# HGRN2 branch of a two-layer hybrid decoder on Trainium2: the local part by doubling blocks of gate products in place of logarithms, scans and exponentials

## Chip, cores and metric

The kernel runs on one NeuronCore of one Trainium2 chip (trn2). Its engines work side by side, each on its own queue of instructions in a fixed order: PE (TensorE: matrix products, with PEld for the loading of their weights), DVE (VectorE), ACT (ScalarE), POOL (GpSimd) and SP (SyncE, which here issues the transfers). The metric is the device time of one execution in microseconds.

## What is computed

The reference is a decoder trunk of two layers on 256 tokens of width 1024. Each layer has a token mixer of three branches (latent attention, gated DeltaNet "dn", HGRN2 "hg"), merged by gates and projected out, and then a mixture of 32 experts. The change lies in the HGRN2 branch of the mixer, which works on 4 heads of 128 channels and in chunks of 64 tokens:

```python
f = lb + (1.0 - lb) * jax.nn.sigmoid(z)
k = (1.0 - lb) * jax.nn.sigmoid(-z)
log_f = jnp.log(jnp.maximum(f, MIN_FORGET))
...
bc = jnp.cumsum(bc, axis=3)
q_dec = qc * jnp.exp(bc)
k_dec = kc * jnp.exp(bc[:, :, :, -1:, :] - bc)
d_last = jnp.exp(bc[:, :, :, -1, :])
...
def step(state, inp):
    dec = masked_exp(tri_incl, bs[:, :, :, None, :] - bs[:, :, None, :, :])
    att = jnp.einsum('bhid,bhjd,bhijd->bhij', qs, ks, dec)
    o = jnp.einsum('bhcd,bhde->bhce', qd, state) + jnp.einsum('bhij,bhje->bhie', att, vs)
    state = state * dl[..., :, None] + jnp.einsum('bhcd,bhce->bhde', kd, vs)
```

The decay between tokens j and i of a chunk is the product of the gates f from j+1 to i, channel by channel. `att` is needed for every pair in a chunk; `q_dec`, `k_dec` and `d_last` hold the products from the chunk's start to a token, from a token to the chunk's end, and over the whole chunk.

## The kernel before

All products are in fp32. Large projections are split into three products of high and low parts: ACT casts a quarter or half of a 1 MB weight tile to its high part `wh` (L249, 128x1024), DVE forms the low part `wl` (L250; at a few places POOL does), and PE runs lines 261, 262 and 263 into a PSUM bank. Activations of the branch are held with channels on partitions and 4 heads x 256 tokens in a row of 1024.

Each layer calls its stages in the order of the string `seq`: `dn_decay`, `mla`, heads, `dn_keys`, `dn_inverse`, `dn_queries`, `dn_values`, `hg_forget`, `hg_project`, `hg_local`, `dn_scan`, `hg_scan`; then the input to the experts, `merge_branch` for "a", the gates, `merge_branch` for "b" and "c", `project_out` and `moe`. That is only the order of the text: a scheduler of the framework sets the order in which instructions stand on each engine, so that PE finds the products of one stage (among them `dn_scan`, L951 to L972, and the projections of `merge_branch`, L261 to L263) between those of another. The order is fixed before the kernel runs; an instruction that waits holds up all behind it on its engine.

`hg_local` (L1011) works in halving blocks. It splits f into two ranges, takes two logarithms (L1022, L1023; a set of activation tables is named at L1021), adds them (L1024) and scans them along each chunk (L1027) to the running sum `b`. `pairs` (L1033) forms, for 4 heads and 4 chunks, the 64x64 products of keys and queries on PE (16 matmuls, L1040), and DVE copies the entries that a mask names into `att` (L1042). It is called seven times: for the diagonal, for blocks of one token (with X = f*q, L1046) and for blocks of 32, 16, 8, 4 and 2 tokens. Each of the last five takes a new tile X: POOL subtracts the block's reference from `b` (L1054, L1055, 512 columns each), ACT takes the exponential (L1056), and DVE multiplies the first half by k (L1057) and the second by q (L1058). At the end POOL, ACT and DVE form the keys for the chunk's state in the same way (L1065 to L1067), PE transposes them (L1072) with copies on ACT (L1073), and ACT and DVE form the decayed queries (L1076, L1077) and the chunk's decay (L1075). `hg_scan` then carries the state through the four chunks (L1094 to L1113).

Behind it, the gates' tanh in `merge_branch` stand at L1289. In `moe`, the router takes exponentials (L1438, L1440), and the tokens that each expert gets are gathered on PE (L1573) and evicted by DVE (L1580) and ACT (L1582). `up` (L1623) and `down` (L1656) are the experts' products. The weights of all stages come through one queue, in order, each tile loaded when a buffer is free: four buffers in the mixer, and eighteen more, opened in steps from the moment at which the mixer's own tiles are given up.

Of the kernel before, what the change touches and what calls it, by code (L numbers as in the profile page):

```python
# [10 lines left out]
F32 = mybir.dt.float32  # L11
# [3 lines left out]
AF = mybir.ActivationFunctionType  # L15
OP = mybir.AluOpType
# [3 lines left out]
DEPTH, D, T = 2, 1024, 256  # L20
# [4 lines left out]
NH = 4  # L25
C = 64
# [81 lines left out]
class Trunk:  # L108
# [357 lines left out]
    def mixer_consts(self, l, mp):  # L466

        nc = self.nc
        self.mconst = mp.tile([128, HOST.shape[1] - KEPT], F32, name="mconst")
        nc.sync.dma_start(self.mconst, self.A["consts"][:, KEPT:])  # L470
        self.ones_r = mp.tile([128, 128], F32R, name="ones")
        one = self.buf("d4", [128, 8, 128])[:, 0]
        nc.gpsimd.memset(one, 1.0)
        nc.gpsimd.tensor_copy(self.ones_r, one)
        self.ones = self.ones_r.bitcast(F32)
        self.scanm = mp.tile([128, T], F32, name="scanm")
        nc.gpsimd.memset(self.scanm, 1.0)
        nc.gpsimd.memset(self.scanm.rearrange("p (n c) -> p n c", c=C)[:, :, 0:1], 0.0)


    def norm_weights(self, l):
# [81 lines left out]
    def router_sums(self, after):  # L563
# [6 lines left out]
        with self.tc.issue_after(after):  # L570
            nc.vector.tensor_reduce(self.rsum, rw.rearrange("p k c -> p c k"), axis=AX.X, op=OP.add)
        nc.vector.tensor_add(self.rsum[0:1, 36:72], self.rsum[0:1, 36:72], self.rb)
# [438 lines left out]
    def hg_local(self, l, mp):  # L1011
        nc = self.nc
        q, k, v, f = self.hq, self.hk, self.hv, self.hf
        fl = lambda x: x.rearrange("p h t -> p (h t)")
        t4 = lambda: self.buf("a4", [128, NH, T])

        lo, g = t4(), t4()
        two60 = 2.0 ** -60
        nc.vector.tensor_scalar(lo, f, 1e-30, two60, op0=OP.max, op1=OP.min)
        nc.vector.tensor_scalar(g, f, two60, None, op0=OP.max)  # L1020
        self.tc.keep_in_program_order(nc.scalar.preload_act_table_set("natural_log_exp_and_others"))  # L1021
        nc.scalar.activation(lo, lo, AF.Ln, scale=2.0 ** 60)  # L1022
        nc.scalar.activation(g, g, AF.Ln)  # L1023
        nc.vector.tensor_add(g, g, lo)  # L1024
        b = t4()
        for h in range(NH):
            nc.vector.tensor_tensor_scan(b[:, h], self.scanm, g[:, h], 0.0, op0=OP.mult, op1=OP.add)  # L1027

        att = self.buf("a2", [128, 8, C])
        nc.gpsimd.memset(att, 0.0)  # L1030
        up, eye = self.cst("uplev"), self.cst("eye64")

        def pairs(xk, xq, m):  # L1033
            ps = self.ps()
            pv = ps.rearrange("p (a i) -> p a i", i=C)
            for t in range(TB):
                for h in range(NH):
                    for c in range(2):
                        o = 128 * t + 64 * c
                        nc.tensor.matmul(pv[64 * c:64 * c + 64, 4 * t + h], xk[:, h, o:o + 64], xq[:, h, o:o + 64],  # L1040
                                         start=True, stop=True)
            nc.vector.copy_predicated(att, m.bitcast(I32)[:, None, :].to_broadcast([128, 8, C]), pv)  # L1042

        pairs(k, q, eye)
        X = t4()
        nc.vector.scalar_tensor_tensor(X, f, 1e-30, q, op0=OP.max, op1=OP.mult)  # L1046
        pairs(k, X, up[:, 0:64])
        for lev in range(5, 0, -1):
            w = 1 << lev
            sp = lambda x: fl(x).rearrange("p (n s w) -> p n s w", s=2, w=w)  # L1050
            X = t4()
            nb = NH * T // (2 * w)
            ref = sp(b)[:, :, 0, w - 1:w].to_broadcast([128, nb, w])
            nc.gpsimd.tensor_tensor(sp(X)[:, :, 0], ref, sp(b)[:, :, 0], op=OP.subtract)  # L1054
            nc.gpsimd.tensor_tensor(sp(X)[:, :, 1], sp(b)[:, :, 1], ref, op=OP.subtract)  # L1055
            nc.scalar.activation(X, X, AF.Exp)  # L1056
            nc.vector.tensor_mul(sp(X)[:, :, 0], sp(X)[:, :, 0], sp(k)[:, :, 0])  # L1057
            nc.vector.tensor_mul(sp(X)[:, :, 1], sp(X)[:, :, 1], sp(q)[:, :, 1])  # L1058
            pairs(X, X, up[:, 64 * lev:64 * lev + 64])
        self.hatt = att  # L1060

        ch = lambda x: fl(x).rearrange("p (n c) -> p n c", c=C)
        last = ch(b)[:, :, C - 1:C]
        X = t4()
        nc.gpsimd.tensor_tensor(ch(X), last.to_broadcast([128, 16, C]), ch(b), op=OP.subtract)  # L1065
        nc.scalar.activation(X, X, AF.Exp)
        nc.vector.tensor_mul(X, X, k)  # L1067
        self.hkd = self.buf("a4", [128, 8, 128])
        for t in range(TB):
            ps = self.ps()  # L1070
            for h in range(NH):
                nc.tensor.transpose(ps[:, 128 * h:128 * h + 128], X[:, h, 128 * t:128 * t + 128], self.ident)  # L1072
            nc.scalar.copy(self.hkd[:, 4 * t:4 * t + 4].rearrange("p h d -> p (h d)"), ps)  # L1073
        self.hdl = self.small([128, 16])
        nc.scalar.activation(self.hdl, last.rearrange("p n c -> p (n c)"), AF.Exp)  # L1075
        nc.scalar.activation(b, b, AF.Exp)  # L1076
        nc.vector.tensor_mul(b, b, q)  # L1077
        self.hqd = b

    def hg_scan(self, l, mp):  # L1080
        nc = self.nc
# [714 lines left out]
```

## Time and profile before

| | us |
|---|---|
| median of three runs | 1173.57 (1173.55 to 1175.22) |
| the profiled execution, its own time | 1175.78 |
| its span, first to last instruction | 1174.0 |
| PE busy (share of the span) | 1070.1 (91%) |
| DVE busy | 592.7 (50%) |
| ACT busy | 450.8 (38%) |
| POOL busy | 178.0 (15%) |
| mean granted TensorE clock | 0.961 of full |

The profile is of one execution. Its times are microseconds from the start of the span unless they are in ns; L1040 is line 1040 of the kernel. A row of the time line gives start, duration, engine, line, operation and tiles, the count of instructions merged into it, and in brackets how long the engine sat idle before it and what ended that. A matmul's duration overlaps with the next one's, so the cost of one is read from the distance between two starts. An fp32 matmul mostly leaves two records. The profile's own "chain that ended last" holds the last 1% of the span alone, so the argument below goes by PE's waits and time lines.

### The profile page before, as it was taken

What the parts mean: (1) busy time and instruction counts of PE and PEld (TensorE: products, weight loads), DVE (VectorE), ACT (ScalarE), POOL (GpSimd) and SP (SyncE); (2) the same over time, 40 slices, a digit from 0 to 9 for tenths busy, and PEclk for the clock granted to TensorE, in tenths of its full rate; (3) what the DMA queues carried; (4) which work ended last, traced back from release to release, by engine and by line L of the source; (5) the groups of instructions that cost most, each with busy time, mean ns of one, the idle gap of its engine ahead of it and who ended that gap; (6) DMA issues with size and microseconds to landing.
All of it is one profiled execution on the core that took longest, in us unless ns stands there. A gap on an engine that the chain in (4) does not pass through costs nothing. (4 is left out here: it accounts for less than half of the span.)

```text
span 1174.0 us, 21469 instructions
## 1 busy us (share of the span) xinstructions
PE 1070.1 (91%) x8896; PEld 776.0 (66%) x8896; DVE 592.7 (50%) x1281; ACT 450.8 (38%) x812; POOL 178.0 (15%) x160
## 2 busy tenths in 40 slices
PE   7999998999999999777899999899999999978775
PEld 5888976777777655444388889667777775644342
DVE  7687648466556323111176775665754563321114
ACT  5764653454444212111077545446444442211111
POOL 2111016401110400000030110470012104000001
PEclk9999998999999999889799999999999999998988
DMA  7631331358985899999983224214499669999995
GB/s 232 199 110 61 109 108 37 122 173 306 419 341 216 335 425 424 427 426 427 399 227 113 74 73 137 80 37 147 159 399 427 233 247 427 424 426 426 427 427 207
DMA packets 104706, 305.58 MB, mean 260 GB/s; under 512 B 20962, under 2 KB 48028, under 8 KB 79516
## 3 DMA queue, kind: packets, MB, share of 16 engines
q1 hardware_dynamic: 104604, 304.15, 67.5%
q8 instruction: 72, 1.18, 0.4%
q14 instruction: 30, 0.25, 0.1%
HBM read 303.08 MB, written 1.05 MB: 259 GB/s over the span
## 5 line engine op out<-in xcount | busy, mean ns | idle before, releaser
L250 DVE TENSOR_TENSOR wl<-w,wh 128x1024 fp32r<-128x1024 f32 x150 | 187.2, 1249 | 157.7 <-ACT wh L249 155.1
L249 ACT CAST wh<-w 128x1024 fp32r<-128x1024 f32 x158 | 165.7, 1049 | 202.5 <-PE ps_pa L263 70.2
L1623 PE MATMUL ps_pa<-w,xg 128*32 128x256 f32 x2304 | 176.7, 437 | 57.2 <-DMA w<-in_exp_w_up_dram 28.3
L1623 PEld LDWEIGHTS ps_pa<-w,xg 128*32 128x32 f32 x2304 | 85.5, 125 | 142.6 <-DMA w<-in_exp_w_up_dram 37.5
L1635 DVE SCALAR_TENSOR_TENSOR hm<-ps_pa,ws,hm 128x256 f32<-128x256 f32 x18 | 8.7, 484 | 203.0 <-ACT hm L1634 202.8
L1634 ACT ACTIVATE hm<-ps_pa 128x256 f32<-128x256 f32 x18 | 6.9, 384 | 221.8 <-PE ps_pa L1623 221.8
L261 PE MATMUL ps_po<-wh,hTh 128*128 128x512 f32 x176 | 71.5, 406 | 2.1 <-ACT hTh L254 0.8
L261 PE MATMUL ps_pa<-wh,hTh 128*128 128x512 f32 x176 | 71.5, 406 | 2.1 <-ACT hTh L254 0.8
L262 PE MATMUL ps_pa<-wl,hTh 128*128 128x512 f32 x176 | 71.1, 404 | 2.1 <-DVE wl L250 1.6
L262 PE MATMUL ps_po<-wl,hTh 128*128 128x512 f32 x176 | 70.9, 403 | 2.1 <-DVE wl L250 1.6
L1656 PE MATMUL ps_pm<-w,hmT 128*32 128x512 f32 x576 | 70.8, 595 | 1.3 <-issue 1.3
L263 PE MATMUL ps_pa<-wh,hTl 128*128 128x512 f32 x176 | 70.9, 403 | 0.2 <-DVE hTl L255 0.2
L263 PE MATMUL ps_po<-wh,hTl 128*128 128x512 f32 x176 | 70.6, 401 | 0.2 <-DVE hTl L255 0.2
L1573 PEld LDWEIGHTS ps_pm<-P,h1c 128*128 128x128 f32 x576 | 66.8, 192 | 2.2 <-ACT res L1371 1.0
L1573 PE MATMUL ps_pm<-P,h1c 128*128 128x128 f32 x576 | 67.4, 275 | 0.1
L1582 ACT ACTIVATE xg<-ps_pm,gb 128x128 f32<-128x128 f32 x72 | 32.9, 458 | 74.7 <-DVE xg L1580 74.7
L1595 POOL TENSOR_TENSOR Pw<-P,small 128x128 f32<-128x128 f32 x32 | 12.4, 406 | 308.2 <-PE ps_pm L1602 231.7
L1300 POOL TENSOR_TENSOR mix<-mix,sg 128x512 f32<-128x512 f32 x16 | 28.3, 1789 | 155.4 <-DVE sg L1298 155.4
L1580 DVE TENSOR_SCALAR xg<-ps_pm,gb 128x128 f32<-128x128 f32 x72 | 29.4, 408 | 41.1 <-PE ps_pm L1573 32.2
L263 PE MATMUL ps_po<-hTh,wl 128*128 128x256 f32 (+1 forms) x168 | 48.8, 290 | 0.8 <-DVE wl L250 0.5
L263 PE MATMUL ps_pa<-hTh,wl 128*128 128x256 f32 (+1 forms) x168 | 48.9, 291 | 0.5 <-DVE wl L250 0.5
L261 PE MATMUL ps_pa<-hTh,wh 128*128 128x256 f32 (+1 forms) x168 | 49.3, 294 | 0.0
(460 smaller groups left out, 2198.1 us busy)
## 6 DMA issues: line engine op xcount, KB each, us to landing
w<-in_exp_w_gate_dram SPq DMA_DIRECT2D x66, 1024.0 KB
w<-in_exp_w_up_dram SPq DMA_DIRECT2D x66, 1024.0 KB
w<-in_exp_w_down_dram SPq DMA_DIRECT2D x64, 1024.0 KB
w<-in_w_in_dram SPq DMA_DIRECT2D x58, 1024.0 KB
w<-in_w_out_dram SPq DMA_DIRECT2D x8, 1024.0 KB
w<-in_w_br_a_dram SPq DMA_DIRECT2D x4, 1024.0 KB
w<-in_w_br_b_dram SPq DMA_DIRECT2D x4, 1024.0 KB
w<-in_w_br_c_dram SPq DMA_DIRECT2D x4, 1024.0 KB
```

Source lines behind the costliest of these rows:

```text
L249: nc.scalar.copy(v(hi), raw)
L250: engine.tensor_tensor(v(lo), raw, v(hi).bitcast(F32), op=OP.subtract)
L261: mm(ps, a[0], b[0], start=start, stop=False, skip_group_check=True)
L262: mm(ps, a[0], b[1], start=False, stop=False, skip_group_check=True)
L263: mm(ps, a[1], b[0], start=False, stop=stop, skip_group_check=True)
L1300: nc.gpsimd.tensor_tensor(mv, mv, sg[t], op=OP.add)
L1573: nc.tensor.matmul(ps[:, 128 * k:128 * k + 128], xc[:, t, 4 * h + k], Ps[q][:, t], start=(t == 0), stop=(t == 1))
L1580: nc.vector.tensor_scalar(xg[:, k], o, g, b, op0=OP.mult, op1=OP.add)
L1582: nc.scalar.activation(xg[:, k], o, AF.Identity, scale=g, bias=b)
L1595: self.pool_last = nc.gpsimd.tensor_tensor(e(Pw[:, t]), e(P[:, t]), w, op=OP.mult)
L1623: nc.tensor.matmul(pg[32 * e:32 * e + 32, FF * n:FF * n + FF], xgs[q][k // 4][:, k % 4, 32 * e:32 * e + 32], w[:, FF * k:FF * k + FF], sta ...
L1656: nc.tensor.matmul(ps[c][32 * e:32 * e + 32], hmT[:, i, 32 * e:32 * e + 32], ws[e][:, D * i + 512 * c:D * i + 512 * c + 512], start=(i == ...
```

## The change

Logarithms, scan and exponentials are gone. Two tiles are kept and grown in place: X starts as q*f and `k` as it is. After the products of a level with blocks of w tokens, POOL multiplies the first half of each pair of blocks in `k` by the gate product of the second block, and DVE multiplies the second half in X by that of the first block; then DVE forms the products `d` for blocks of twice the length. The levels run from 1 to 32 tokens, smallest first. After six of them X is `q_dec`, k is `k_dec` and the last `d` is the chunk's decay. `f` is clamped below once, in place. The number of `pairs` calls (seven) and of PE instructions stays. The set of tables for logarithm and exponential is no longer loaded here. In the changed file the products are at L1025, the masked copy at L1027, the clamp at L1031, X = q*f at L1034, POOL's product at L1044, DVE's at L1045, `d` at L1047 and the transposes at L1056.

```diff
@@ -473,9 +473,6 @@
         nc.gpsimd.memset(one, 1.0)
         nc.gpsimd.tensor_copy(self.ones_r, one)
         self.ones = self.ones_r.bitcast(F32)
-        self.scanm = mp.tile([128, T], F32, name="scanm")
-        nc.gpsimd.memset(self.scanm, 1.0)
-        nc.gpsimd.memset(self.scanm.rearrange("p (n c) -> p n c", c=C)[:, :, 0:1], 0.0)
 
 
     def norm_weights(self, l):
@@ -1014,18 +1011,6 @@
         fl = lambda x: x.rearrange("p h t -> p (h t)")
         t4 = lambda: self.buf("a4", [128, NH, T])
 
-        lo, g = t4(), t4()
-        two60 = 2.0 ** -60
-        nc.vector.tensor_scalar(lo, f, 1e-30, two60, op0=OP.max, op1=OP.min)
-        nc.vector.tensor_scalar(g, f, two60, None, op0=OP.max)
-        self.tc.keep_in_program_order(nc.scalar.preload_act_table_set("natural_log_exp_and_others"))
-        nc.scalar.activation(lo, lo, AF.Ln, scale=2.0 ** 60)
-        nc.scalar.activation(g, g, AF.Ln)
-        nc.vector.tensor_add(g, g, lo)
-        b = t4()
-        for h in range(NH):
-            nc.vector.tensor_tensor_scan(b[:, h], self.scanm, g[:, h], 0.0, op0=OP.mult, op1=OP.add)
-
         att = self.buf("a2", [128, 8, C])
         nc.gpsimd.memset(att, 0.0)
         up, eye = self.cst("uplev"), self.cst("eye64")
@@ -1041,41 +1026,35 @@
                                          start=True, stop=True)
             nc.vector.copy_predicated(att, m.bitcast(I32)[:, None, :].to_broadcast([128, 8, C]), pv)
 
+
+
+        nc.vector.tensor_scalar(f, f, 1e-30, None, op0=OP.max)
         pairs(k, q, eye)
-        X = t4()
-        nc.vector.scalar_tensor_tensor(X, f, 1e-30, q, op0=OP.max, op1=OP.mult)
-        pairs(k, X, up[:, 0:64])
-        for lev in range(5, 0, -1):
+        X, rest = t4(), t4()
+        nc.vector.tensor_mul(X, q, f)
+        self.hdl = self.small([128, 16])
+        d, at = fl(f), 0
+        for lev in range(6):
             w = 1 << lev
+            pairs(k, X, up[:, 64 * lev:64 * lev + 64])
+            n = NH * T // (2 * w)
             sp = lambda x: fl(x).rearrange("p (n s w) -> p n s w", s=2, w=w)
-            X = t4()
-            nb = NH * T // (2 * w)
-            ref = sp(b)[:, :, 0, w - 1:w].to_broadcast([128, nb, w])
-            nc.gpsimd.tensor_tensor(sp(X)[:, :, 0], ref, sp(b)[:, :, 0], op=OP.subtract)
-            nc.gpsimd.tensor_tensor(sp(X)[:, :, 1], sp(b)[:, :, 1], ref, op=OP.subtract)
-            nc.scalar.activation(X, X, AF.Exp)
-            nc.vector.tensor_mul(sp(X)[:, :, 0], sp(X)[:, :, 0], sp(k)[:, :, 0])
-            nc.vector.tensor_mul(sp(X)[:, :, 1], sp(X)[:, :, 1], sp(q)[:, :, 1])
-            pairs(X, X, up[:, 64 * lev:64 * lev + 64])
+            d2 = d.rearrange("p (n s) -> p n s", s=2)
+            over = lambda s: d2[:, :, s, None].to_broadcast([128, n, w])
+            nc.gpsimd.tensor_tensor(sp(k)[:, :, 0], sp(k)[:, :, 0], over(1), op=OP.mult)
+            nc.vector.tensor_tensor(sp(X)[:, :, 1], sp(X)[:, :, 1], over(0), op=OP.mult)
+            dn = self.hdl if lev == 5 else fl(rest)[:, at:at + n]
+            nc.vector.tensor_tensor(dn, d2[:, :, 0], d2[:, :, 1], op=OP.mult)
+            d, at = dn, at + n
         self.hatt = att
 
-        ch = lambda x: fl(x).rearrange("p (n c) -> p n c", c=C)
-        last = ch(b)[:, :, C - 1:C]
-        X = t4()
-        nc.gpsimd.tensor_tensor(ch(X), last.to_broadcast([128, 16, C]), ch(b), op=OP.subtract)
-        nc.scalar.activation(X, X, AF.Exp)
-        nc.vector.tensor_mul(X, X, k)
+        self.hqd = X
         self.hkd = self.buf("a4", [128, 8, 128])
         for t in range(TB):
             ps = self.ps()
             for h in range(NH):
-                nc.tensor.transpose(ps[:, 128 * h:128 * h + 128], X[:, h, 128 * t:128 * t + 128], self.ident)
+                nc.tensor.transpose(ps[:, 128 * h:128 * h + 128], k[:, h, 128 * t:128 * t + 128], self.ident)
             nc.scalar.copy(self.hkd[:, 4 * t:4 * t + 4].rearrange("p h d -> p (h d)"), ps)
-        self.hdl = self.small([128, 16])
-        nc.scalar.activation(self.hdl, last.rearrange("p n c -> p (n c)"), AF.Exp)
-        nc.scalar.activation(b, b, AF.Exp)
-        nc.vector.tensor_mul(b, b, q)
-        self.hqd = b
 
     def hg_scan(self, l, mp):
         nc = self.nc
```

**On PE, first layer, around the last levels.** L1040 (before) and L1025 (now) are the products of `pairs`; L948, L956, L957 and L962 now (L951, L959, L960 and L965 before) belong to `dn_scan`; `hTh`/`hTl` rows are the projection of the first merge gate. Before, the groups for blocks of 32, 16, 8 and 4 tokens:

```order
L262 MATMUL ps_pa<-wl,hTh 128x512
L1040 MATMUL ps_pm<-a_2003 64x64 x16
L1040 MATMUL ps_pm<-a_2027 64x64 x16
L263 MATMUL ps_pa<-wh,hTl 128x512
L261 MATMUL ps_pa<-wh,hTh 128x512
L262 MATMUL ps_pa<-wl,hTh 128x512
L1040 MATMUL ps_pm<-a_2051 64x64 x16
L263 MATMUL ps_pa<-wh,hTl 128x512
L262 MATMUL ps_po<-wl,hTh 128x512
L263 MATMUL ps_po<-wh,hTl 128x512
L261 MATMUL ps_po<-wh,hTh 128x512
L1040 MATMUL ps_pm<-a_2075 64x64 x16
```

Now, the groups for 16 and 32 tokens and the transposes:

```order
L948 MATMUL ps_pb<-d_2148,d_1552 64x128 x4
L956 MATMUL ps_pb<-d_2148,d_1581 64x128
L262 MATMUL ps_po<-wl,hTh 128x512
L263 MATMUL ps_po<-wh,hTl 128x512
L1025 MATMUL ps_pm<-a_1968,a_1619 64x64 x16
L957 MATMUL ps_pb<-d_2151,d_1262 64x128
L956 MATMUL ps_pb<-d_2148,d_1581 64x128
...
L957 MATMUL ps_pb<-d_2151,d_1262 64x128
L1025 MATMUL ps_pm<-a_1968,a_1619 64x64 x16
L962 MATMUL ps_pb<-d_2151,d_744 128x128 x3
L1056 MATMUL ps_pm<-const,a_1619 128x128 x8
```

Before, two groups of `pairs` stood together and one to four products of the projection between the others; now most of `dn_scan` stands between them, and three matmuls stand between the last group and the transposes.

**On DVE, first layer, the first levels.** The masked copy is L1042 before and L1027 now. Before:

```order
L250 TENSOR_TENSOR wl<-w,wh 128x1024
L1042 COPY_PREDICATED a_1963<-mconst,ps_pm 128x512
L1057 TENSOR_TENSOR a_2003<-a_2003,a_1622 128x16x32
L1058 TENSOR_TENSOR a_2003<-a_2003,a_1754 128x16x32
L1057 TENSOR_TENSOR a_2027<-a_2027,a_1622 128x32x16
L1058 TENSOR_TENSOR a_2027<-a_2027,a_1754 128x32x16
L1057 TENSOR_TENSOR a_2051<-a_2051,a_1622 128x64x8
L1042 COPY_PREDICATED a_1963<-mconst,ps_pm 128x512
L1058 TENSOR_TENSOR a_2051<-a_2051,a_1754 128x64x8
```

Now:

```order
L1047 TENSOR_TENSOR a_1969<-a_1969 128x128
L250 TENSOR_TENSOR wl<-w,wh 128x1024
L1027 COPY_PREDICATED a_1947<-mconst,ps_pm 128x512
L1045 TENSOR_TENSOR a_1968<-a_1968,a_1620 128x512
L1047 TENSOR_TENSOR a_1969<-a_1969 128x64
...
L1045 TENSOR_TENSOR a_1968<-a_1968,a_1969 128x256x2
L950 TENSOR_TENSOR d_2126<-d_1551,ps_pb 64x512
L250 TENSOR_TENSOR wl<-w,wh 128x1024
L1027 COPY_PREDICATED a_1947<-mconst,ps_pm 128x512
L1045 TENSOR_TENSOR a_1968<-a_1968,a_1969 128x128x4
```

Now each masked copy stands ahead of the in-place product of X (L1045) that the next group on PE needs, and at two levels L250, the low part of the next projection's weights, stands ahead of both.

**On ACT, at the router of the first layer.** Before:

```order
L1371 ACTIVATE res<-res,small,ln_rs 128x512 x4
L1438 ACTIVATE small<-small 128x4
L1440 ACTIVATE small<-small 128x1
L1438 ACTIVATE small<-small 128x4
L1440 ACTIVATE small<-small 128x1
L1582 ACTIVATE xg<-ps_pm,gb_281 128x128 x4
L1634 ACT_TABLE_LOAD
```

Now:

```order
L1350 ACTIVATE res<-res,small,ln_rs 128x512 x4
L1417 ACT_TABLE_LOAD
L1417 ACTIVATE small<-small 128x4
L1419 ACTIVATE small<-small 128x1
L1417 ACTIVATE small<-small 128x4
L1419 ACTIVATE small<-small 128x1
L1561 ACTIVATE xg<-ps_pm,gb_278 128x128 x4
L1613 ACT_TABLE_LOAD
```

A load of activation tables now stands ahead of the router's exponentials (L1417, L1419; before L1438, L1440). In the mixer three loads are gone: at L1021, L1022 and L1289. The second layer has the same orders.

## Rows read from the trace of the kernel before

**Rows 1.** What the transfers moved, 40 equal slices of the span.

```profile
GB/s 232 199 110 61 109 108 37 122 173 306 419 341 216 335 425 424 427 426 427 399 227 113 74 73 137 80 37 147 159 399 427 233 247 427 424 426 426 427 427 207
```

**Rows 2.** PE's waits, layer 0, 160 to 220: who for whom, total, times, longest.

```profile
PE ps_pm L1040 <- DVE a L1058: 2.9, 2, 1.9
PE ps_pm L1040 <- DVE a L1046: 1.3, 1, 1.3
PE ps_pm L1094 <- ACT a L1073: 0.3, 1, 0.3
PE ps_pa L261 <- ACT sg L1289: 0.2, 1, 0.2
```

**Rows 3.** The same, layer 1, 738 to 796; the other three as in layer 0.

```profile
PE ps_pm L1040 <- DVE a L1058: 4.2, 4, 1.9
```

**Rows 4.** Two windows: busy time of PE, PEld, DVE, ACT, POOL; PEclk; DMA; GB/s.

```profile
182.90:194.10 11.20, 8.30 (x102) 6.85 (x102) 10.05 (x11) 4.47 (x5) 10.91 (x8) 0.54 0.14 52
...
759.30:767.70 8.40, 5.50 (x68) 4.47 (x67) 7.25 (x8) 3.51 (x4) 8.40 (x6) 0.59 0.18 69
```

**Rows 5.** PE's time line, layer 0.

```profile
172.14 0.43 PE L960 MATMUL ps_pb<-d,d 64*64 64x128 f32 x2
172.50 1.16 PE L965 MATMUL ps_pb<-d,d 64*128 64x128 f32 x8
173.58 0.50 PE L263 MATMUL ps_po<-wh,hTl 128*128 128x512 f32 x1
173.92 0.40 PE L261 MATMUL ps_po<-wh,hTh 128*128 128x512 f32 x1
174.15 0.40 PE L262 MATMUL ps_po<-wl,hTh 128*128 128x512 f32 x1
...
188.02 1.98 PE L1040 MATMUL ps_pm<-a 128*64 128x64 f32 x32 [1.03 <-DVE a L1058]
189.93 0.80 PE L263 MATMUL ps_pa<-wh,hTl 128*128 128x512 f32 x1
...
191.51 1.98 PE L1040 MATMUL ps_pm<-a 128*64 128x64 f32 x32
...
194.82 1.15 PE L1040 MATMUL ps_pm<-a 128*64 128x64 f32 x32
...
217.58 0.49 PE L261 MATMUL ps_pa<-wh,o 128*128 128x512 f32 x1 [0.24 <-ACT sg L1289]
```

**Rows 6.** DVE's time line, layer 0.

```profile
165.00 0.73 DVE L1042 COPY_PREDICATED a<-mconst,ps_pm 128x512 f32<-128x512 int32 x1 [3.37 <-POOL wl L250]
...
176.71 1.20 DVE L1046 SCALAR_TENSOR_TENSOR a<-a,a 128x1024 f32<-128x1024 f32 x1
...
186.25 1.63 DVE L1058 TENSOR_TENSOR a<-a,a 128x512 f32<-128x512 f32 x1
...
194.47 1.73 DVE L1057 TENSOR_TENSOR a<-a,a 128x512 f32<-128x512 f32 x1
196.12 0.68 DVE L1058 TENSOR_TENSOR a<-a,a 128x512 f32<-128x512 f32 x1
```

**Rows 7.** POOL's time line, layer 0.

```profile
178.77 2.05 POOL L1055 TENSOR_TENSOR a<-a 128x512 f32<-128x512 f32 x1
180.78 1.03 POOL L971 TENSOR_TENSOR d<-d,small 128x512 f32<-128x512 f32 x1
...
185.74 1.59 POOL L1055 TENSOR_TENSOR a<-a 128x512 f32<-128x512 f32 x1
```

**Rows 8.** ACT's time line, layer 0: a table load, and the router's end.

```profile
166.24 1.28 ACT L1021 ACT_TABLE_LOAD   x1
167.53 1.06 ACT L1023 ACTIVATE a<-a 128x1024 f32<-128x1024 f32 x1
...
379.97 0.46 ACT L1582 ACTIVATE xg<-ps_pm,gb 128x128 f32<-128x128 f32 x1 [1.36 <-DVE xg L1580]
```

**Rows 9.** PE's waits, experts of layer 0, 372 to 572.

```profile
PE ps_pa L1623 <- DMA w<-in_exp_w_gate_dram: 14.7, 9, 1.8
```

## Prediction

> **What bounds the kernel now.** Begin with the engines' shares: PE is busy for 91% of the span, so only what keeps PE waiting or slow can be worth much. Next, what the transfers moved [rows 1]: they run at the most that this trace shows (424 to 427 GB/s) in the stages of the experts and far below it in the mixer. The change lies in the mixer, twice (164 to 218 in layer 0, 740 to 794 in layer 1). There PE's waits are the view to read [rows 2, 3]. In layer 0 PE waits 1.3 us for X = f*q (L1046, which stands behind the scan on DVE), 2.9 us for the products of the levels (L1058), 0.3 for the copy behind the transposes and 0.2 for the tanh behind its table load: 4.7 in all. In layer 1 the waits for L1058 are 4.2 and the rest as before: 6.0.
>
> Then the granted clock [rows 4]: after those waits it is 0.54 of full over 11.2 us and 0.59 over 8.4 us, that is for most of each window at the lower of its two levels (1.2 of 2.4 GHz). What that costs is seen on the time line [rows 5]: a group of `pairs` that lasts 1.15 us at 194.82 lasts 1.98 at 188.02 and at 191.51, 0.83 more. Three groups lie in the slow stretch of layer 0 (2.5 us), and three projection products between 189.93 and 191.51 take 1.58 us where 0.9 would do (0.23 each, 0.1 at each change of kind). With a fifth of a microsecond of others: 3.3 us. Layer 1 by the shorter window, 8.4 of 11.2: 2.5.
>
> So the local part costs PE 8.0 us in layer 0 and 8.5 in layer 1, in waits and low clock. It does so because everything waits for the scan, and because POOL then spends two subtractions a level.
>
> **What goes.** On ACT two logarithms, six full exponentials and a seventh for the queries (1.06 us each, the row at 167.53 [rows 8]) and three table loads of 1.28; on DVE the scan, the sum and 12 products; on POOL eleven subtractions. None of that counts by itself, since only PE's waits and clock were on the path: it is worth the 8.0 and 8.5.
>
> There is a third term, in the order on PE. Between the last ten products for the diagonal and the first product of the branch projection PE changes 25 times between large projection products and small ones before, and 11 times now. A change costs 0.1 us: 173.58 to 173.92 is 0.34, 173.92 to 174.15 is 0.23 [rows 5]. That is 14 times 0.1, 1.3 rounded down. PE's instructions are the same in number and shape, so nothing else changes there.
>
> **What comes: a closed loop.** Before, a level's X was a new tile and levels overlapped. Now `k` and X are grown in place: POOL and DVE may write only when PE has read the level's group, and the next group needs what they wrote. A round on DVE is: a lag (0.14: L1058 at 186.25 ends at 187.88, the group on PE starts at 188.02 [rows 5, 6]), the masked copy, which stands first in DVE's order (0.73), the product of X, a lag again. The product has no row; the nearest are DVE's two-input products over 512 columns, 0.68 alone and up to 1.73 beside POOL [rows 6]. I take 1.1, between them, since POOL works at the same moment. Round: 0.14 + 0.73 + 1.1 + 0.14 = 2.1 us, bounds 1.7 and 2.75. On POOL the product of `k` is bounded by 1.03 and 2.05 [rows 7]; I take 1.5, a round of 1.8, so X is the later one.
>
> What stands on PE between the groups covers this. Unit costs [rows 5]: 0.36 for one matmul of the alternating `dn_scan` rows (172.14 to 172.50), 1.08 for four others (172.50 to 173.58), 0.23 for a projection product. Counted in the new order: after the level of 1 token 2.9 us, of 2 tokens 3.0, of 4 tokens 5.4, of 8 tokens 1.8 (four, one and two products), of 16 tokens 2.5 (seven alternating), and of 32 tokens 0.8 (three, at a quarter of 1.08). Against a round of 2.1 the waits are:
> - after 1 token, 0.4: L250 stands ahead of the masked copy and adds 1.2 (as large as L1046, 1.20 [rows 6]), 3.3 against 2.9;
> - after 2, 4 and 16 tokens none; after 4 tokens L250 stands ahead again, and waits for a cast on ACT that waits for PE, but 5.4 covers the two;
> - after 8 tokens, 0.3;
> - before the transposes, 1.0: 1.8 for POOL's last product against 0.8;
> - behind the transposes, 0.3 for the ACT copy, as now.
>
> Together 2.0 us a layer. With the lower bounds 0.5 (the transposes alone), with the upper ones 4.0 (1.1, 0.95, 0.2, 1.5 and 0.3).
>
> The head of the chain is hidden: X = q*f takes what L1046 took (1.20) and the first `d` products under 1 us each, where DVE sat 3.37 us before the copy at 165.00 [rows 6]. The clamp of f costs less than L1046 and stands behind `hg_forget`, 20 us ahead of its reader; if it delayed L250 there, PE would lose under 1.2. The later `d` are narrower; I cost them at nothing beside the covers above. No transfer moves past another: SP's order is the same, and each weight tile is released by its split, which comes earlier now.
>
> **The load that moves to the router.** The tanh of the merge now runs on the set already loaded, and the router's exponentials need a load of 1.28 us (L1021's row [rows 8]) instead. The eviction of gathered tokens on ACT stands behind it. Before, ACT sat 1.36 us ahead of that for DVE [rows 8], and DVE's new order has other work there first. So I charge 0.15 a layer; uncovered it would be 1.28. The Trainium skill, "ScalarE: Activation LUTs", section "What ACT_TABLE_LOAD costs", gives 1.28 us for the load and 1.38 more for a drain, 2.66 for a switch. This trace shows the load but not the drain: L1023 starts 1.29 us behind it [rows 8]. By the page the router would lose up to 1.3 us a layer more and the time would be 2.6 us longer.
>
> **Sum.** Layer 0: 8.0 + 1.3 - 2.0 = 7.3. Layer 1: 8.5 + 1.3 - 2.0 = 7.8. Less 0.3 for the routers: 14.8 us. What comes behind is the same work in the same order, and its weights are asked for when the mixer's tiles are given up, which moves with PE; so the gain passes through. Against the profiled execution (1175.78): 1161.0. It lies 2.2 above the median of the runs (1173.57), against which I give the number: **1158.8**. With all lower bounds and no loss at the router: 15.1 + 2 x 1.5 = 18.1, 1155.5. With all upper ones (waits of 4.0, router 1.28): 15.1 - 4.0 - 2.6 = 8.5, 1165.1.
>
> **Rivals.**
> - *DVE and POOL take strict turns.* At 185.74 POOL's subtraction takes 1.59 and DVE's product, started at 186.25, ends only at 187.88, 0.55 behind it; alone they take 1.03 and 0.68 [rows 6, 7]. If each simply waits the other out, a round is 0.14 + 1.03 + 0.68 + 0.14 = 2.0 with the masked copy hidden under POOL, and POOL's last product is over in 1.3; the waits fall to 0.1 + 0.2 + 0.5 + 0.1 = 0.9, and the time to 1158.8 - 2.2 = 1156.6. Against it: other rows beside POOL last up to 1.73. The Trainium skill, "SBUF — State Buffer", section "SBUF: two separate sides", states this as a rule: the two engines share a port pair as an exclusive lock, taken for a whole instruction, also by a DVE operation with two SBUF inputs. The rows above agree.
> - *The clock falls all the same.* If the waits after 1 and 8 tokens and ahead of the transposes leave PE at the lower level as now, the 3.3 and 2.5 are paid again, and some 1 more since all groups follow closer: 1158.8 + 7 = 1165.8. For it: a single wait of 1.9 preceded the fall [rows 2]. Against it: my longest is 1.0, and the wait of 1.3 at L1046 left the clock full.
> - *The expert weights swallow it.* Transfers run at 424 to 427 GB/s through most of the experts [rows 1], and PE waits 14.7 us for one kind of weight tile alone [rows 9]. If their stream started at a time of its own, an earlier mixer would only wait longer: 1173.6. Against it: ahead of that stretch they fall to 216 GB/s in a slice, so the buffers are full and the stream resumes when PE frees them.
> - *Slower: the closed loop becomes the bound.* If the in-place products cost their upper rows one after the other (0.73 + 1.73 + 2.05 and two lags, 4.8 a round), PE waits 3.1 + 1.8 + 0 + 3.0 + 2.3 + 3.3 = 13.5 a layer, with six groups at low clock 5.0 more: 18.5 against 9.3 gained, 2 x 9.2 slower, 1192. It decides from a round of about 3.8 us on at full clock, 2.9 with the clock low. Nothing in the rows adds these three up.
>
> **How the numbers follow.** The forecast has 0.55, strict turns 0.20, the low clock 0.13, the swallowed gain 0.07, the closed loop 0.05. The range reaches from 1155.5 to 1166.4: the sum's bounds (1155.5 to 1165.1), which hold strict turns too, and the low clock at 1165.8; it leaves out the last two cases. About 0.2% (2.3 us) can be told from no change: faster is 0.55 + 0.20 + 0.13 = 0.88, same 0.07, slower 0.05.
>
> **What would show it.** PE's waits for L1045 and L1044 should sum to about 1.7 us a layer, the longest ahead of the transposes; the clock should be full from 164 to 210; the first product of the branch projection, at 217.58 now [rows 5], should start near 210; the first expert product should be 7 us earlier in layer 0 and 15 in layer 1. It would be wrong if DVE's round were above 2.75, if the clock fell in spite of short waits, or if PE's waits for expert weights grew by what the mixer saved.

## The result, and the profile after

| | before | after |
|---|---|---|
| device time, median of 4 runs each (lowest, highest) | 1173.69 us (1173.55, 1175.22) | 1158.54 us (1156.85, 1160.61) |
| ratio, with its 95% interval | | 0.9868 (0.9856 to 0.9880) |
| profiled execution: its time, its span | 1175.78, 1174.0 | 1160.61, 1158.8 |

The change makes the kernel 15.15 us faster; 14.8 was forecast. The total hides two errors of opposite sign, so the time line is read in stages first. Each stage is the distance between two starts of rows: POOL's split L250 near 162 (and near 732 in layer 1) and the first branch product on PE (the local part); DVE's L337 and the first projection product, both at the start of layer 1; and the end of the span.

| stage, us | before | after | gain |
|---|---|---|---|
| to POOL's split near 162 | 162.51 | 162.30 | 0.21 |
| local part, layer 0 | 55.07 | 45.69 | 9.38 |
| from there to L337 of layer 1 | 372.24 | 371.03 | 1.21 |
| start of layer 1, L337 to first projection product | 6.78 | 11.35 | **-4.57** |
| from there to POOL's split of layer 1 | 142.31 | 141.96 | 0.35 |
| local part, layer 1 | 55.07 | 45.69 | 9.38 |
| to the end | 380.02 | 380.78 | -0.76 |

The local part gained 2.1 us more than forecast in layer 0 and 1.6 in layer 1. And 4.57 us were given back where the change seems to do nothing. (The third row is no gain of the change: an experiment below with before's order took 370.36 there.)

First the local part. PE's waits of after, layer 0, 160 to 220, answer to [rows 2]:

```profile
PE ps_pm L1056 <- POOL a L1044: 0.4, 1, 0.4
PE ps_pb L948 <- DVE d L969: 0.3, 1, 0.3
PE ps_pm L1025 <- DVE a L1047: 0.3, 1, 0.3
PE ps_pm L1025 <- DVE a L1045: 0.2, 1, 0.2
PE ps_pa L261 <- DVE mix L1277: 0.2, 1, 0.2
```

The local part itself has the upper four, 1.2 us, the longest ahead of the transposes (L1056). Next the two windows of the local part, of before and of after: stretch, its length, busy time and instructions of PE, PEld, DVE, ACT and POOL, granted clock, DMA share, GB/s.

```profile
162.51:217.58 55.07, 50.15 (x456) 36.52 (x455) 35.01 (x38) 24.88 (x31) 35.10 (x21) 0.91 0.17 56
```

```profile
162.30:207.99 45.69, 44.49 (x456) 33.97 (x455) 24.14 (x31) 11.58 (x17) 27.98 (x16) 1.00 0.17 58
```

The same 456 matmuls: before, PE sat idle for 4.92 us and was busy for 50.15 at a clock of 0.91; now it is idle for 1.20 and busy for 44.49 at full clock. The window that stood at 0.54 [rows 4] stands at 1.00 now:

```profile
182.90:194.10 11.20, 10.48 (x124) 7.77 (x119) 5.62 (x8) 1.65 (x3) 2.94 (x4) 1.00 0.01 1
```

On the time line, the first expert product of before:

```profile
381.20 0.63 PE L1623 MATMUL ps_pa<-w,xg 128*32 128x256 f32 x6
```

and, of after, the first branch product (217.58 before [rows 5]) and the first expert product:

```profile
207.99 0.39 PE L261 MATMUL ps_pa<-wh,o 128*128 128x512 f32 x1
...
371.38 1.93 PE L1602 MATMUL ps_pa<-w,xg 128*32 128x256 f32 x31
```

The expert product comes 9.82 us earlier, so nothing was lost on the way through the router. On ACT there, the new load and the eviction behind it:

```profile
368.02 1.28 ACT L1417 ACT_TABLE_LOAD   x1
369.32 0.30 ACT L1417 ACTIVATE small<-small 128x4 f32<-128x4 f32 x1
...
370.14 0.46 ACT L1561 ACTIVATE xg<-ps_pm,gb 128x128 f32<-128x128 f32 x1
```

The eviction is 9.83 earlier than its row before [rows 8]: the load lies in the 1.36 us that ACT sat idle there.

Now the start of layer 1. Before, by engine: POOL's constants and first pooled split, DVE's L338 and the scaled diagonal (L622), PE's products with it, and the first projection product.

```profile
589.70 0.34 POOL L477 MEMSET scanm<- 128x256 f32 x1
589.99 0.29 POOL L474 CAST ones<-d 128x128 fp32r<-128x128 f32 x1
590.22 0.10 POOL L478 MEMSET scanm<- 128x4 f32 x1
590.39 2.36 POOL L250 TENSOR_TENSOR wl<-w,wh 128x1024 fp32r<-128x1024 f32 x1
...
590.31 0.16 DVE L338 SCALAR_TENSOR_TENSOR ln_tmp<-ln_tmp 128x2 f32<-128x2 f32 x1
...
592.07 0.95 DVE L622 TENSOR_SCALAR sg<-const,ln_rs 128x128 f32<-128x128 f32 x2 [0.61 <-DVE ln_rs L344]
...
593.04 2.02 PE L395 MATMUL ps_pm<-sg,res 128*128 128x128 f32 x16 [0.20 <-PE ps_pa L365]
...
596.60 0.36 PE L261 MATMUL ps_pm<-hTh,wh 128*128 128x256 f32 x1
```

After:

```profile
579.19 0.29 POOL L474 CAST ones<-d 128x128 fp32r<-128x128 f32 x1
579.47 2.35 POOL L250 TENSOR_TENSOR wl<-w,wh 128x1024 fp32r<-128x1024 f32 x1
582.54 2.34 POOL L250 TENSOR_TENSOR wl<-w,wh 128x1024 fp32r<-128x1024 f32 x1 [0.72 <-ACT wh L249]
...
579.50 2.34 DVE L338 SCALAR_TENSOR_TENSOR ln_tmp<-ln_tmp 128x2 f32<-128x2 f32 x1
...
583.10 2.07 DVE L619 TENSOR_SCALAR sg<-const,ln_rs 128x128 f32<-128x128 f32 x2 [0.26 <-DMA mconst<-in_consts_dram]
...
585.17 3.03 PE L395 MATMUL ps_pm<-sg,res 128*128 128x128 f32 x16 [3.02 <-issue]
...
590.37 0.36 PE L261 MATMUL ps_pm<-hTh,wh 128*128 128x256 f32 x1
```

The diff also takes the two memsets of `scanm` off POOL. Without them POOL's split starts 0.03 us before L338 instead of 0.08 after it, and L338, an instruction on two columns, lasts 2.34 us instead of 0.16: until POOL's split is done. That makes the diagonal late, so that it meets POOL's second split and takes 2.07 instead of 0.95, and PE idles 3.02. The stretch costs PE 2.81 us more idle time and 1.76 more at a lower clock (the granted clock from L337 to the first projection product is 0.85 now and was 1.00, with PE busy 8.34 us against 6.58): 4.57.

So the first theory, A: the loss is this meeting of POOL's split and L338, decided by hundredths of a microsecond. Its rival, B: the late start has another cause and the memsets cost nothing.

### The profile page after: what moved, and what is told of

The parts are those of the page before. It is cut to its first block, busy times and chain, and to the rows that moved or that the text cites. A ratio compares the mean times of both kernels' runs of the same rounds, so it can differ in the third digit from the quotient of the medians.

```text
span 1158.8 us, 21407 instructions
## 1 busy us (share of the span) xinstructions
PE 1059.3 (91%) x8896; PEld 775.6 (67%) x8896; DVE 576.9 (50%) x1269; ACT 427.3 (37%) x788; POOL 162.7 (14%) x146
## 5 line engine op out<-in xcount | busy, mean ns | idle before, releaser
L250 DVE TENSOR_TENSOR wl<-w,wh 128x1024 fp32r<-128x1024 f32 x150 | 187.0, 1248 | 161.5 <-ACT wh L249 161.0
L1602 PEld LDWEIGHTS ps_pa<-w,xg 128*32 128x32 f32 x2304 | 88.0, 125 | 140.4 <-DMA w<-in_exp_w_up_dram 38.2
```

The source lines that it names most:

```text
L250: engine.tensor_tensor(v(lo), raw, v(hi).bitcast(F32), op=OP.subtract)
L1602: nc.tensor.matmul(pg[32 * e:32 * e + 32, FF * n:FF * n + FF], xgs[q][k // 4][:, k % 4, 32 * e:32 * e + 32], w[:, FF * k:FF * k + FF], sta ...
```

## The experiments

Each was timed in 4 or 5 runs beside runs of the kernel before on the same chip, whose medians were 1173.95 (e1 to e4) and 1174.18 (e5 to e7); the ratios are to those. The stages that the edits touch:

| | median us | ratio (95%) | local, layer 0 | start of layer 1 | local, layer 1 |
|---|---|---|---|---|---|
| before | 1173.69 | | 55.07 | 6.78 | 55.07 |
| after | 1158.54 | 0.9868 (0.9856 to 0.9880) | 45.69 | 11.35 | 45.69 |
| e1, memsets back | 1154.25 | 0.9838 (0.9825 to 0.9851) | 45.69 | 6.78 | 45.69 |
| e2, other form of L338 | 1155.37 | 0.9838 (0.9825 to 0.9852) | 45.69 | 6.50 | 45.69 |
| e3, before, memsets later | 1178.92 | 1.0041 (1.0027 to 1.0055) | 55.06 | 11.35 | 55.05 |
| e4, k's products on DVE | 1156.12 | 0.9847 (0.9833 to 0.9860) | 44.16 | 11.19 | 44.15 |
| e5, X's product twice | 1164.53 | 0.9914 (0.9900 to 0.9928) | 49.89 | 11.25 | 46.85 |
| e6, e2 and e4 | 1151.48 | 0.9806 (0.9792 to 0.9820) | 44.15 | 6.67 | 44.15 |
| e7, before, all on DVE | 1189.35 | 1.0131 (1.0115 to 1.0147) | 62.64 | 6.92 | 63.87 |

**e1: the memsets back.**

```diff
         self.ones = self.ones_r.bitcast(F32)
+        self.scanm = mp.tile([128, T], F32, name="scanm")
+        nc.gpsimd.memset(self.scanm, 1.0)
+        nc.gpsimd.memset(self.scanm.rearrange("p (n c) -> p n c", c=C)[:, :, 0:1], 0.0)
```

> The changed kernel with the two memsets of scanm (which nothing reads any more) put back on POOL in mixer_consts; the order on PE, DVE, ACT and SP is that of the changed kernel. Theory A (at the start of layer 1 POOL's first pooled split, L250, begins 0.03 us before DVE's two-input L338 on 128x2 and holds it for 2.3 us, and the second split then holds the scaled diagonal; this gave back 4.4 us): the memsets put POOL's split 0.4 to 0.8 us later, L338 is done in 0.16 us again, the layer starts 10.6 us earlier than before instead of 6.2, and the time is 1158.5 - 4.4 = 1154.1 us (1153 to 1155.5). Rival B (the memsets cost nothing and the late start has another cause, the transfer of the constants or PE's clock): 1158.5, within 0.7 us.

Measured: 1154.25 us; two instructions whose result nobody reads make the changed kernel 4.3 us faster by the medians, 3.5 by the ratios. DVE's and POOL's rows:

```profile
577.92 0.16 DVE L338 SCALAR_TENSOR_TENSOR ln_tmp<-ln_tmp 128x2 f32<-128x2 f32 x1
...
577.82 0.10 POOL L478 MEMSET scanm<- 128x4 f32 x1
577.99 2.36 POOL L250 TENSOR_TENSOR wl<-w,wh 128x1024 fp32r<-128x1024 f32 x1
```

L338 is 0.07 us ahead again, and the start of layer 1 is at 6.78, as before. Theory A holds, B falls.

**e2: L338 in the form of its neighbours.**

```diff
-        nc.vector.scalar_tensor_tensor(tmp, tmp, -10.0 / 3, tmp, op0=OP.add, op1=OP.mult)
+        for t in range(TB):
+            ts(tmp[:, t], tmp[:, t], -10.0 / 3, tmp[:, t], op0=OP.add, op1=OP.mult)
```

> The changed kernel with L338, one scalar_tensor_tensor on 128x2 with two tensors from SBUF, written as two tensor_scalar on 128x1 with a column as the second scalar, the form of the lines around it; no other instruction moves. Theory A in its narrow form (POOL's running tensor_tensor holds only those DVE instructions that read two tensors from SBUF): the two take 0.2 to 0.4 us beside POOL's split, the diagonal is made before the second split, 1154.1 us (1153 to 1155.5). Wide form (any DVE instruction is held while POOL's tensor_tensor runs): the first of the two takes the 2.3 us, 1158.5. Rival B (another cause of the late start): 1158.5, within 0.7 us.

Measured: 1155.37 us, at the upper end of what the narrow form expected: 3.2 us faster by the medians, 3.5 by the ratios, where the stretch itself gained 4.85 in the profiled execution. POOL's split and DVE's rows behind it:

```profile
579.18 2.36 POOL L250 TENSOR_TENSOR wl<-w,wh 128x1024 fp32r<-128x1024 f32 x1
...
579.26 0.33 DVE L339 TENSOR_SCALAR ln_tmp<-ln_tmp 128x1 f32<-128x1 f32 x2
579.50 0.34 DVE L341 TENSOR_SCALAR ln_rs<-ln_tmp,ln_rs 128x1 f32<-128x1 f32 x2
579.75 0.45 DVE L343 TENSOR_SCALAR ln_tmp<-ln_rs,ln_v 128x1 f32<-128x1 f32 x2
580.12 0.33 DVE L345 TENSOR_SCALAR ln_rs<-ln_tmp,ln_rs 128x1 f32<-128x1 f32 x2
580.71 1.10 DVE L620 TENSOR_SCALAR sg<-const,ln_rs 128x128 f32<-128x128 f32 x2 [0.26 <-DVE ln_rs L345]
```

POOL starts 0.08 us ahead and runs until 581.54, and eight one-column `tensor_scalar` with the second operand as a column pass beside it at their usual length. So not all of DVE is held: L338's form with two tensors from SBUF is, the one-column form is not (a wider form with one tensor is held too, see the last section). The rule of the Trainium skill ("SBUF — State Buffer", "SBUF: two separate sides") agrees: between a POOL instruction and a DVE instruction with two inputs from SBUF, the pair of ports that the two engines share goes as a lock to whichever starts first, for its whole instruction.

**e3: the mirror image, in the kernel before.**

```diff
-        nc.gpsimd.memset(self.scanm, 1.0)
-        nc.gpsimd.memset(self.scanm.rearrange("p (n c) -> p n c", c=C)[:, :, 0:1], 0.0)
...
         b = t4()
+        with self.tc.issue_after(self.latest(nc.gpsimd)):
+            nc.gpsimd.memset(self.scanm, 1.0)
+            nc.gpsimd.memset(self.scanm.rearrange("p (n c) -> p n c", c=C)[:, :, 0:1], 0.0)
         for h in range(NH):
```

> The kernel before with nothing but the two memsets of scanm moved from mixer_consts to just before the scans, behind POOL's work of that time; the order on every other engine is that of before. Theory A: POOL's first pooled split of layer 1 now begins 0.4 to 0.8 us earlier, at or just ahead of L338 as in the changed kernel, and holds it: about 4 us slower than before, 1177.5 us (1176 to 1179); if it comes a few hundredths of a us after L338 instead, 1173.7. Rival B: 1173.7, within 0.7 us.

Measured: 1178.92, 5.0 us slower than before, and the start of layer 1 takes 11.35 us as in the changed kernel.

```profile
588.45 2.36 POOL L250 TENSOR_TENSOR wl<-w,wh 128x1024 fp32r<-128x1024 f32 x1
...
588.48 2.34 DVE L338 SCALAR_TENSOR_TENSOR ln_tmp<-ln_tmp 128x2 f32<-128x2 f32 x1
```

The loss can be had without the change, and the change without the loss (e1, e2): the two are independent.

**e4: the products on k on DVE.** The second question is the local part: does POOL's share buy anything when it takes turns with DVE? In the changed kernel, layer 0, DVE's masked copies and products on X, and POOL's products on k:

```profile
170.74 1.32 DVE L1045 TENSOR_TENSOR a<-a,a 128x512 f32<-128x512 f32 x1
...
183.75 0.73 DVE L1027 COPY_PREDICATED a<-mconst,ps_pm 128x512 f32<-128x512 int32 x1 [0.74 <-PE ps_pm L1025]
184.37 1.11 DVE L1045 TENSOR_TENSOR a<-a,a 128x512 f32<-128x512 f32 x1
...
187.99 1.08 DVE L1045 TENSOR_TENSOR a<-a,a 128x512 f32<-128x512 f32 x1
...
170.21 1.30 POOL L1044 TENSOR_TENSOR a<-a,a 128x512 f32<-128x512 f32 x1 [1.99 <-issue]
...
183.86 1.07 POOL L1044 TENSOR_TENSOR a<-a,a 128x512 f32<-128x512 f32 x1 [0.55 <-PE ps_pm L1025]
187.47 1.05 POOL L1044 TENSOR_TENSOR a<-a,a 128x512 f32<-128x512 f32 x1 [2.54 <-PE ps_pm L1025]
```

In all three the product on X ends 0.55 us behind POOL's (172.06 and 171.51, 185.48 and 184.93, 189.07 and 188.52). The layer's other three rounds end 0.54 or 0.55 us apart too, though in two of them X began 1.7 and 1.8 us after POOL, and not 0.5 as here: turns.

```diff
-            nc.gpsimd.tensor_tensor(sp(k)[:, :, 0], sp(k)[:, :, 0], over(1), op=OP.mult)
+            nc.vector.tensor_tensor(sp(k)[:, :, 0], sp(k)[:, :, 0], over(1), op=OP.mult)
```

> The changed kernel with the six in-place products on k on DVE as well instead of POOL (POOL has none of the local part's products left; PE's and DVE's orders are planned anew around it). Strict turns (POOL's and DVE's products never overlap, so that POOL's share buys nothing): DVE does a pair in about the 2.1 us that the pair of POOL and DVE takes now, the local part keeps its length within 1 us and the time is 1158.5, within 1.5 us. The rival that POOL's product really runs beside DVE's: each round is longer by DVE's 0.9 to 1.1 us, of which PE has no other work for all, 6 rounds x 2 layers x 0.5 to 1 = 6 to 12 us slower, 1164 to 1170.

Measured: 1156.12, 2.4 us faster than after: not the rival, and below the theory's range (1157 to 1160) as well.

```profile
185.65 0.73 DVE L1027 COPY_PREDICATED a<-mconst,ps_pm 128x512 f32<-128x512 int32 x1 [0.85 <-PE ps_pm L1025]
186.27 0.67 DVE L1044 TENSOR_TENSOR a<-a,a 128x512 f32<-128x512 f32 x1
186.86 0.68 DVE L1045 TENSOR_TENSOR a<-a,a 128x512 f32<-128x512 f32 x1
```

With no POOL beside it a product lasts 0.67 or 0.68. Copy and both products take 1.89 us (185.65 to 187.54) where copy and one product beside POOL took 1.73 (183.75 to 185.48): POOL's share saved 0.16 of a round. That alone makes e4 no faster. What does is the window of its local part:

```profile
162.00:206.16 44.16, 44.16 (x456) 33.80 (x455) 23.34 (x37) 11.59 (x17) 13.55 (x9) 1.00 0.21 70
```

PE has no gap left. The order on PE was planned anew around the new DVE work, and it now has projection products ahead of the transposes, where after waits 0.4 us for POOL. How much of the 1.53 us a layer is the order and how much the engine was not separated.

**e5: the closed loop made longer.**

```diff
             nc.vector.tensor_tensor(sp(X)[:, :, 1], sp(X)[:, :, 1], over(0), op=OP.mult)
+            nc.vector.tensor_tensor(sp(junk)[:, :, 1], sp(X)[:, :, 1], over(0), op=OP.mult)
```

> The changed kernel with the product on X made a second time in each level, into a tile that nothing reads, right behind the first on DVE: 0.68 us more for each of the twelve rounds (the orders are planned anew around it). By the closed loop of the prediction the rounds that PE's other work does not cover (after 1, 8 and 16 tokens) cost 1.5 to 2.5 us a layer more, the granted clock stays full, and the time is 1161.5 to 1163.5. Rival 1 (the loop has slack everywhere, since the extra product is not in the chain from one level to the next): 1158.5, within 1. Rival 2 (PE's waits pass the point at which the clock falls, as before the change): 5 us a layer more on top, 1170 to 1174.

Measured: 1164.53, 1 us above the first range, far below the third. But the layers differ: the local part grew by 4.20 us in layer 0 and by 1.16 in layer 1. The window of layer 1, and three of layer 0:

```profile
736.37:783.22 46.85, 46.16 (x456) 34.12 (x455) 28.93 (x38) 11.47 (x17) 26.30 (x15) 1.00 0.19 65
```

```profile
184.00:186.00 2.00, 2.00 (x13) 1.08 (x12) 2.00 (x3) 0.02 (x1) 1.96 (x1) 1.00 0.00 0
186.00:188.00 2.00, 2.00 (x9) 1.54 (x9) 1.55 (x3) 0.55 (x1) 0.00 (x0) 0.58 0.03 8
188.00:190.00 2.00, 2.00 (x33) 1.79 (x32) 0.34 (x1) 0.00 (x0) 0.00 (x0) 0.50 0.00 0
```

In layer 0 the clock falls to its lower level (1.2 of 2.4 GHz) at about 186 and stays there until about 193; in layer 1 it stays full, with the same instructions. So the fall cost 3.04 us here (49.89 less 46.85). The loop itself is not tested at the order of after: in the order planned anew PE sits idle for 0.69 us of layer 1's window, less than after's 1.20, and what is added is busy time (46.16 against 44.49). The first window serves as a scale for another term. Its order on PE changes 26 times between large projection products and small ones, as often as before's (counted on the same stretch, 162.51 to 217.58), where after's changes 12 times. At full clock PE is busy for 46.16 us there and for 44.49 in after: 1.67 for 14 changes, 0.12 each. The scale is rough: e4's order changes 16 times and is busy for 44.16, less than after's, so a window's busy time holds more than its changes.

**e6: e2 and e4 together.**

> The edits of e2_form (L338 as two tensor_scalar) and e4_alldve (the products on k on DVE) together in the changed kernel. Theory: they act in different places and add. e4_alldve took 1.53 us off each of the two local parts (44.16 instead of 45.69 us from POOL's split to the first product of the branch projection), e2_form 4.85 off the start of layer 1 (6.50 instead of 11.35 us from L337 to the first projection product): 1158.5 - 3.1 - 4.85 = 1150.6 us (1149 to 1152.5). Rival (they are two ways to the same gain, for instance because both only move POOL's split against DVE): no better than the better of the two, 1155 to 1156.

Measured: 1151.48 us, ratio 0.9806 (0.9792 to 0.9820). They add: the local parts are e4's, the start of layer 1 is within 0.17 us of e2's. It is the fastest version, 7 us ahead of the changed kernel.

**e7: the kernel before without POOL in the local part.** This asks whether turns, and not the logarithms and scans, were the loss before.

```diff
-            nc.gpsimd.tensor_tensor(sp(X)[:, :, 0], ref, sp(b)[:, :, 0], op=OP.subtract)
-            nc.gpsimd.tensor_tensor(sp(X)[:, :, 1], sp(b)[:, :, 1], ref, op=OP.subtract)
+            nc.vector.tensor_tensor(sp(X)[:, :, 0], ref, sp(b)[:, :, 0], op=OP.subtract)
+            nc.vector.tensor_tensor(sp(X)[:, :, 1], sp(b)[:, :, 1], ref, op=OP.subtract)
...
-        nc.gpsimd.tensor_tensor(ch(X), last.to_broadcast([128, 16, C]), ch(b), op=OP.subtract)
+        nc.vector.tensor_tensor(ch(X), last.to_broadcast([128, 16, C]), ch(b), op=OP.subtract)
```

> The kernel before with the eleven subtractions of the local part on DVE instead of POOL, all else of the logarithms, scans and exponentials kept (the orders are planned anew around it). Theory C (the loss of the local part before, 10.9 us against the 44.16 of e4_alldve, lies in the amount of work for a level and in the scan ahead of it): DVE then does 2 subtractions, 2 products at 0.68 and a masked copy at 0.73, 3.45 us a level, as long as the 3.49 between two groups before, so the local part stays within 1.5 us of 55.07 and the time is 1173.9, within 3. Rival D (the loss is that POOL and DVE take turns on SBUF, and putting all on one engine mends it without the change): the local part falls towards 46 to 48, 1156 to 1160 us. Another rival: DVE is overloaded, 1177 or more.

Measured: 1189.35, 15 us slower; theory C missed as D did. PE's waits, 158 to 228:

```profile
PE ps_pm L1040 <- DVE a L1058: 9.7, 4, 2.7
PE ps_pm L1040 <- DVE a L1046: 2.1, 1, 2.1
```

and DVE's own waits, 165 to 205, its first and those for PE's groups:

```profile
DVE a L1042 <- POOL wl L250: 3.4, 1, 3.4
...
DVE a L1042 <- PE ps_pm L1040: 1.1, 3, 0.4
```

From the scan to the last group DVE waits for PE for 1.1 us in all, and PE up to 2.7 us at a time for DVE, where the longest was 1.9 [rows 2]: DVE is the bound there. The same move, POOL's share to DVE, costs the old computation 7.6 us in layer 0 (55.07 to 62.64) and gains the new one 1.53. So D falls: putting the work on one engine does not mend the old computation. With POOL's share on POOL the old one takes 9.38 us more than the new one in layer 0, with all on DVE 18.48 (62.64 less 44.16): the loss goes with the computation that the change takes out. Two things are not shown: that turns cost nothing in before (a DVE product beside POOL lasts up to 1.73 us there, alone 0.68 [rows 6]), and how much of the loss is the logarithms and the scan ahead of the levels and how much the work of a level.

## Why the prediction was right, and where it was wrong

**The local part: right in what goes and what comes, with the sizes off and two terms not separate.** The forecast was a gain of 7.3 us in layer 0; it is 9.38.
- PE's waits before: 4.7 taken from the list, 4.92 idle in the window.
- The low clock: 3.3. PE was busy 50.15 us in before and is busy 46.16 in e5's layer 1, at full clock and with as many changes of kind: 4.0.
- The order on PE: 1.3. It is 1.67, by the same rough scale; 0.1 for a change was 0.12.
- The new waits: 2.0. They are 1.20: 0.4 ahead of the transposes instead of 1.0, none behind them instead of 0.3, and about as said after 1 and 8 tokens (0.3 and 0.2); 0.3 in `dn_scan` (L948) was not foreseen.

Together 4.92 + 4.0 + 1.67 - 1.20 = 9.4. That sum has to come out, since a window's idle and busy time make up its length: 3.72 us less idle and 5.66 less busy are measured, and the split of the 5.66 rests on e5's window.

In layer 1 the gain is the same 9.38 against 7.8. There the waits in the list were longer and the low clock shorter [rows 3, 4], and the local part came to the same 55.07 us. So did both layers of e3 (55.06 and 55.05), with PE idle for 5.94 and 6.19 us at a clock of 0.94, where layer 0 of before has 4.92 at 0.91. This is what the prediction had wrong here: it added waits and low clock as two losses, but where the clock was low for less time, PE waited that much longer. What set the length there is then the chain through POOL, ACT and DVE for which PE waited (POOL was busy for 10.91 of 11.20 us and for all of 8.40 in the two slow stretches [rows 4]); no run has the kernel before at full clock throughout. In e5, where PE hardly waits, the low clock did cost its 3.04 us.

**What the views were to show** came out: clock full from 164 on, first branch product at 207.99 (near 210 was said), longest wait ahead of the transposes. The first expert product is 9.82 us earlier in layer 0 (7 was said) and 16.22 in layer 1 (15). The waits for L1045 and L1044 are 0.6, or 0.9 with the one put down to L1047, which stands right behind X's product; 1.7 was said.

**The router**: 0.15 was charged a layer, nothing was paid, and the load is 1.28 us. The drain that the Trainium skill ("ScalarE: Activation LUTs", "What ACT_TABLE_LOAD costs") adds is not seen: L1417's first exponential starts 1.30 us behind the load's start, and the load starts 0.02 us behind the end of the instruction ahead of it on ACT (L1350, until 368.00).

**"So the gain passes through"** is the step that failed, and it failed on an edit that had no line of its own in the sum: the memsets. What they did, delaying what stood behind them on POOL, was never asked. Their removal cost 4.57 us on the profiled stretch, and 3.2 to 5.0 in the times of e1, e2 and e3. That the total fell within 0.3 us of 1158.8 is luck: the local parts gained 3.66 more than forecast (2.08 and 1.58), and this gave back 4.57. Without the loss the time is e1's, 1154.25, below the range's low end: the range had no case for what happened.

**The rivals.** *Strict turns* had a chance of 0.20, yet it is the better account of the products: each on X ends 0.55 us behind POOL's, as the row at 186.25 had shown [rows 6, 7]. Its price for the waits, 0.9, is nearer the measured 1.2 (0.9 without L948's) than the forecast's 2.0. The same rule, applied to all pairs of POOL and DVE that the change shifts, could have led to the start of layer 1. *The clock falls* did not happen in the changed kernel's local parts, and did in one layer of e5. *The expert weights swallow it* fell: PE waits 15.4 and 13.4 us for the two kinds of expert weight in layer 0, 28.8 in all, where it waited 14.7 [rows 9] and 14.3. *The closed loop* was far off: in after, copy and product take 1.73 us (183.75 to 185.48), 2.0 with the two lags of 0.14, where it needed a round of 3.8.

## What to carry to other kernels

Cost what an edit removes by what stood behind it on its engine, too: a dead instruction can be the delay that lets two others miss each other. Where POOL and DVE both work, look for DVE instructions with two tensors from SBUF on the critical chain next to long POOL instructions, however small they are, and give them another form: e2's two lines took 4.85 us off a stretch, about half of what the whole change took off one local part. And measure the loss of a stretch as its window's idle time plus its busy time beyond that of the same instructions undisturbed; the list of waits alone gave 4.7 us where 10.9 could be won (55.07 less e4's 44.16).

## What was not expected of the hardware

- A DVE instruction on 128x2 lasted 2.34 us instead of 0.16 because POOL's 2.35 us instruction had begun 0.03 us earlier; with DVE 0.07 or 0.08 us ahead (e1, before) neither lost anything that shows.
- The diagonal, a `tensor_scalar` on 128x128 with one tensor, is held as well: beside POOL's second split its first half lasts 1.87 us and its second 0.28. The one-column ones are not (e2).
- In e5 the granted clock fell at about 186 in layer 0 although PE had no wait above 0.28 us from 162 on and was busy for all of the 2 us ahead, while the same instructions in layer 1 kept it full. In before it was full from 172.00 to 182.90, with the wait of 1.3 us for L1046 [rows 2] in that stretch. So the longest single wait, by which the prediction judged this rival, does not tell when it falls; what does stays open.
